# Two-channel stores, smaller early loads and a 5 to 4 split of copies in an im2col kernel

## The chip, the cores and the metric

The kernel runs on one core of a Trainium2 chip. The metric is device microseconds of one execution. A run is "fast" when it was within 1.5% of the fastest run of the same kernel, "slow" when it was longer, and "unknown" when it was the only one. The span in a profile is shorter than the time by about 1.8 us (90.1 and 91.84 us for the same run of the kernel before).

## The reference

```python
x: (16, 64, 32, 32) float32, kernel_size = 3
cols = zeros(16, 64 * 9, 30 * 30)
for b: for i in range(30): for j in range(30):
    cols[b, :, i * 30 + j] = x[b, :, i:i+3, j:j+3].ravel()
```

Each channel of 32 x 32 becomes nine windows of 30 x 30. 4.19 MB are read and 33.18 MB are written; nothing is computed.

## The kernel before

Each of the 128 partitions holds 8 channels, 32 KB in one row of `x`. Loads and stores are done by 16 DMA engines, which move rows between the chip's main memory and the on-chip memory. A channel's nine windows are copied inside the on-chip memory, by VectorE and ScalarE, into an output tile (32.4 KB per channel), and a store writes the tile's row out. Two output tiles of two channels each alternate.

```python
    cuts = [0, H, 200, CPP * H]              # rows: 4, 21 and 7 KB per partition
    first = load(nc.sync, cuts[0], cuts[1])
    bulk = load(nc.sync, cuts[1], cuts[2])
    load(nc.sync, cuts[2], cuts[3])

    on_act = (False, True, False, True, False)
    n = 0
    for c in range(0, CPP, 2):
        out_tile = out_pool.tile([P, 2, KK, HO, WO], x.dtype, name="out_tile")
        for s in range(2):
            for kk in range(KK):
                # ... one copy, on ScalarE or VectorE by on_act[n % 5]
            if c == 0:
                st = nc.sync.dma_start(out=out_v[:, s], in_=out_tile[:, s]...)
                if s == 0:
                    tc.add_manual_dep(st.ins, bulk.ins.name, ...)  # store after the bulk load
        if c > 0:
            nc.sync.dma_start(out=out_v[:, c : c + 2]..., in_=out_tile...)
```

## Time and profile before

| | before |
|---|---|
| median of 3 runs | 91.53 us (91.47 to 92.0) |
| span of the profiled run | 90.1 us |
| DMA engines busy | 97.0% |
| VectorE, ScalarE busy | 26%, 29% |
| first store issued | 10.50 us |
| last of the three loads landed | 12.6 us (issued at 1.2, 11.4 to landing) |

The lines behind it are in the prediction below. They are read as follows: the DMA share is the bound, and what the copying engines do matters only where it decides when a store can be issued.

Beside the profile's views I use the trace's packet records, one for each row that a DMA engine moved (start, duration, bytes) and one of 4 bytes for each engine's completion of a transfer. They carry no engine number. Where I speak of single engines, I joined records in which one starts as another ends. Each of the 16 engines has 8 of the 128 rows of every transfer.

### The profile page before, as it was taken

What the parts mean: (1) busy time and instruction counts of PE and PEld (TensorE: products, weight loads), DVE (VectorE), ACT (ScalarE), POOL (GpSimd) and SP (SyncE); (2) the same over time, 40 slices, a digit from 0 to 9 for tenths busy, and PEclk for the clock granted to TensorE, in tenths of its full rate; (3) what the DMA queues carried; (4) which work ended last, traced back from release to release, by engine and by line L of the source; (5) the groups of instructions that cost most, each with busy time, mean ns of one, the idle gap of its engine ahead of it and who ended that gap; (6) DMA issues with size and microseconds to landing.
All of it is one profiled execution on the core that took longest, in us unless ns stands there. A gap on an engine that the chain in (4) does not pass through costs nothing.

```text
span 90.1 us, 140 instructions
## 1 busy us (share of the span) xinstructions
DVE 23.5 (26%) x43; ACT 26.2 (29%) x30; POOL 0.2 (0%) x4
## 2 busy tenths in 40 slices
DVE  0380399970000089600000399300000000000000
ACT  5391399940000089920000399300000000000000
POOL 0000000000000000000000000000000000000000
DMA  5999899999599999993799999999999999947990
GB/s 129 486 382 449 360 518 446 460 460 446 259 460 460 691 460 432 460 432 173 345 460 460 460 460 460 460 460 460 460 460 460 460 432 460 403 201 345 460 460 0
DMA packets 1152, 37.37 MB, mean 415 GB/s; under 512 B 128, under 2 KB 128, under 8 KB 384
## 3 DMA queue, kind: packets, MB, share of 16 engines
q1 hardware_dynamic: 1152, 37.37, 97.0%
HBM read 4.19 MB, written 33.18 MB: 415 GB/s over the span
## 4 chain that ended last, share of the span: by engine, by line
DMA 45%; DVE 16%; DVEq 1%; issue 0%; SPq 0%
DMA out_dram<-out_tile 35%; DVE out_tile L57 16%; DMA in_tile<-in_x_dram 11%; DVEq L93 1%; DVEq L57 0%; SPq L75 0%
## 5 line engine op out<-in xcount | busy, mean ns | idle before, releaser
L55 ACT COPY out_tile<-in_tile 128x900 f32<-128x900 f32 x29 | 24.9, 938 | 30.1 <-DMA out_dram<-out_tile 25.3
L57 DVE COPY out_tile<-in_tile 128x900 f32<-128x900 f32 x43 | 23.5, 624 | 33.6 <-DMA out_dram<-out_tile 26.0
L55 ACT ACT_TABLE_LOAD x1 | 1.3, 1283 | 0.8 <-PEq L122 0.8
L122 POOL MEMSET const-bfloat16-1.0<- 128x1 bf16 x1 | 0.1, 102 | 0.0
L122 POOL MEMSET const-uint8-127<- 128x1 uint8 x1 | 0.1, 102 | 0.0
L122 POOL MEMSET const-float32-0.0<- 128x1 f32 x1 | 0.1, 99 | 0.2 <-issue 0.2
L122 POOL MEMSET const-float32-1.0<- 128x1 f32 x1 | 0.1, 99 | 0.0
## 6 DMA issues: line engine op xcount, KB each, us to landing
out_dram<-out_tile SPq DMA_DIRECT2D x3, 8100.0 KB, 31.3
out_dram<-out_tile SPq DMA_DIRECT2D x2, 4050.0 KB, 14.9
in_tile<-in_x_dram SPq DMA_DIRECT2D x1, 2688.0 KB, 9.6
in_tile<-in_x_dram SPq DMA_DIRECT2D x1, 896.0 KB, 11.4
in_tile<-in_x_dram SPq DMA_DIRECT2D x1, 512.0 KB, 3.6
```

The lines of the kernel that those rows point to most:

```text
L55: nc.scalar.copy(out=dst, in_=src)
L57: nc.vector.tensor_copy(out=dst, in_=src)
L93: tc.compile()
L122: nc = _bacc.Bacc("TRN2", target_bir_lowering=False, num_devices=1)
```

## The change

The intent is fewer and larger stores, an earlier start of the second channel (so that a first store of two channels can be ready as early as the old one of one channel), and a split of copies that is the same for each channel.

```diff
-    cuts = [0, H, 200, CPP * H]
-    first = load(nc.sync, cuts[0], cuts[1])
-    bulk = load(nc.sync, cuts[1], cuts[2])
-    load(nc.sync, cuts[2], cuts[3])
+    first = load(nc.sync, 0, H)
+    load(nc.sync, H, 2 * H)
+    load(nc.sync, 2 * H, CPP * H)
-    on_act = (False, True, False, True, False)
+    on_act = (False, True, False, True, False, True, False, True, False)
 ...
-            if c == 0:
-                st = nc.sync.dma_start(... one channel ...)
-                if s == 0:
-                    tc.add_manual_dep(st.ins, bulk.ins.name, ...)
-        if c > 0:
-            nc.sync.dma_start(... two channels ...)
+        nc.sync.dma_start(... two channels ...)
```

(Shortened. An assertion on the number of channels is loosened too; it holds here either way.)

More of the change, by code (lines that the diff above doesn't have):

```diff
@@ L19, in _im2col @@
     CPP = B * C // P
-    assert CPP * P == B * C and C % CPP == 0 and CPP % 4 == 0
+    assert CPP * P == B * C and C % CPP == 0 and CPP % 2 == 0
     x_v = x.rearrange("b (cp c2) h w -> (b cp) (c2 h w)", c2=CPP)
@@ L58, in _im2col @@
                 n += 1
-            if c == 0:
-                st = nc.sync.dma_start(
-                    out=out_v[:, s],
-                    in_=out_tile[:, s].rearrange("p kk i j -> p (kk i j)"),
-                )
-                if s == 0:
-                    tc.add_manual_dep(
-                        st.ins,
-                        bulk.ins.name,
-                        mybir.DependencyInfo(
-                            mybir.DependencyClass.Sync, mybir.DependencyReason.DATA
-                        ),
-                        reason="the store follows the bulk of the loads",
-                    )
-        if c > 0:
-            nc.sync.dma_start(
-                out=out_v[:, c : c + 2].rearrange("p c n -> p (c n)"),
-                in_=out_tile.rearrange("p c kk i j -> p (c kk i j)"),
-            )
+        nc.sync.dma_start(
+            out=out_v[:, c : c + 2].rearrange("p c n -> p (c n)"),
+            in_=out_tile.rearrange("p c kk i j -> p (c kk i j)"),
+        )
     return first
```

## The prediction

> **What bounds the kernel now.** I read the page first, for engine shares and DMA. This is the page of the kernel before.
>
> ```profile
> span 90.1 us, 140 instructions
> DVE 23.5 (26%) x43; ACT 26.2 (29%) x30; POOL 0.2 (0%) x4
> ...
> DMA  5999899999599999993799999999999999947990
> ...
> q1 hardware_dynamic: 1152, 37.37, 97.0%
> HBM read 4.19 MB, written 33.18 MB: 415 GB/s over the span
> ```
>
> The two copying engines are busy about a quarter of the span each; the DMA engines 97% of it. The slices marked 5, 3 and 7 in the middle of the DMA row look like holes. To see whether they are, I asked for stretches whose borders I set by the transfers: loads until 11.5, the one-channel stores until 30.7, then one two-channel store per stretch. Columns: stretch, its length, busy time of each engine, clock, DMA share (1.00 is all 16 engines), GB/s.
>
> ```profile
> 0.00:1.00 1.00, 0.00 (x0) 0.21 (x1) 0.20 (x4) 1.00 0.00 0
> 1.00:11.50 10.50, 3.85 (x7) 5.61 (x7) 0.00 (x0) 1.00 1.01 398
> 11.50:21.10 9.60, 8.16 (x16) 7.47 (x9) 0.00 (x0) 1.00 1.01 434
> 21.10:30.70 9.60, 0.00 (x0) 0.00 (x0) 0.00 (x0) 1.00 1.00 432
> 30.70:49.80 19.10, 5.47 (x10) 6.85 (x8) 0.00 (x0) 1.00 1.00 434
> 49.80:69.00 19.20, 6.01 (x11) 6.01 (x7) 0.00 (x0) 1.00 1.00 432
> 69.00:88.20 19.20, 0.00 (x0) 0.00 (x0) 0.00 (x0) 1.00 1.00 432
> 88.20:90.10 1.90, 0.00 (x0) 0.00 (x0) 0.00 (x0) 1.00 0.00 0
> ```
>
> No hole: a packet is counted where it starts, and packets of the big stores last about 2.4 us, so slices of 2.25 us alternate. The share is 1.00 or 1.01 in every stretch from 1.0 to 88.2 us. The time is 1.0 us ahead of the first packet, 87.2 us of full DMA, and 1.9 us for the last packets' ends and the landing. Only bytes, bytes per second, or a new hole can change the sum. The chain of waits names VectorE for 16% of the span, but that is a path through slack: while VectorE copies, the stretch's DMA share is 1.00.
>
> Next, where the copies and issues stand, from the instructions in order of time (start, length, engine and line, names, count, wait before it):
>
> ```profile
> 3.61 3.48 ACT L55 COPY out_tile<-in_tile 128x900 f32<-128x900 f32 x4 [1.54 <-DMA in_tile<-in_x_dram]
> 3.61 2.78 DVE L57 COPY out_tile<-in_tile 128x900 f32<-128x900 f32 x5 [3.61 <-DMA in_tile<-in_x_dram]
> 10.43 8.54 ACT L55 COPY out_tile<-in_tile 128x900 f32<-128x900 f32 x10 [3.35 <-DMA in_tile<-in_x_dram]
> 10.43 9.23 DVE L57 COPY out_tile<-in_tile 128x900 f32<-128x900 f32 x17 [4.04 <-DMA in_tile<-in_x_dram]
> 10.50 3.67 SPq L60 DMA_DIRECT2D out_dram<-out_tile  x2
> 19.74 37.77 SPq L75 DMA_DIRECT2D out_dram<-out_tile  x3
> 31.95 6.85 ACT L55 COPY out_tile<-in_tile 128x900 f32<-128x900 f32 x8 [12.98 <-DMA out_dram<-out_tile]
> 31.97 5.47 DVE L57 COPY out_tile<-in_tile 128x900 f32<-128x900 f32 x10 [12.31 <-DMA out_dram<-out_tile]
> ```
>
> Channel 0 is copied by 7.1 us, but its store waits for the second load and is issued at 10.50. The pair at 31.95 is done in 6.85 us, because ScalarE has 8 copies there; the issue follows about 0.02 us later.
>
> **What the Trainium skill says.** "DMA: Bandwidth & Descriptors", section "Where 436 GB/s comes from": a fabric ceiling of 435 GB/s; the trace's full stretches run at 432 to 434, so this kernel's stores are at it. The same page, "Queues, rings and completion order": on each DMA engine descriptors are consumed in ring order; the trace agrees in that loads are followed by stores at share 1.00, all on one queue, and a store issued ahead merely queues. "ScalarE: Activation LUTs", "What ACT_TABLE_LOAD costs": an activation with immediates takes 186 + 0.833 N ns and neighbours overlap by about 93 ns. For N = 900 that is 936 ns each, 843 ns apart; the trace shows 938 ns on average and (6.85 - 0.94) / 7 = 0.845 us apart. "VectorE: DVE Perf Modes", "Side-by-side": two fp32 elements per cycle plus about 150 cycles, (450 + 150) / 0.96 = 625 ns; the trace shows 624 ns. So both engines' copies are what they should be, and the change alters none of their shapes.
>
> **The change part by part.**
>
> *Bytes and packets.* The bytes stay 37.37 MB. Loads go from 4, 21 and 7 KB per partition to 4, 4 and 24; all remain contiguous rows of at least 4 KB. Stores go from two of 32.4 KB and three of 64.8 KB per partition to four of 64.8 KB. At the traced rate two one-channel stores take 9.60 + 9.60 = 19.20 us, one two-channel store 19.10 to 19.20, so the merge is worth 0 to 0.1 us. Issues fall from 8 to 7 and packets by 144 (128 rows and 16 completion packets), to 1008; on a queue that is full, issuing costs nothing.
>
> *The first store.* This is the one place with little slack. It now needs two channels, 10 VectorE and 8 ScalarE copies. Channel 0 starts at 3.61 as before. The second load is now 512 KB: at 398 GB/s (the load stretch) 1.3 us after the first, so it lands at about 4.9. VectorE reaches channel 1 at 3.61 + 2.78 = 6.39 and ScalarE at 7.09, so neither waits: the stalls of 3.35 and 4.04 us until 10.43 go. ScalarE ends at 3.61 + 6.85 = 10.46 and VectorE at about 3.61 + 5.47 = 9.1. The store is issued at about 10.5, by chance just when the old first store was. When must it be issued to leave no hole? The first load, issued at 0.0, had its first packets just after 1.0 us, so about 1.0 us passes from issue to data. In the kernel before, in half-microsecond stretches:
>
> ```profile
> 11.00:11.50 0.50, 0.50 (x2) 0.50 (x2) 0.00 (x0) 1.00 1.05 444
> 11.50:12.00 0.50, 0.50 (x2) 0.50 (x1) 0.00 (x0) 1.00 2.34 1001
> ```
>
> A 32.4 KB packet takes 1.2 us (9.60 us for 8 per engine), so 2.34 x 0.5 x 16 / 1.2 = 15.6 means that about one store packet started on each of the 16 engines between 11.5 and 12.0: the loads ended there and stores followed at once. An issue at 10.5 gives data at 11.5, so a hole of 0 to 0.1 us. Its cost is one for one, as nothing later catches up.
>
> *The later stores.* The second pair needs the third load, whose bytes end as before and which lands at about 12.6 (1.2 + 11.4 us). Its copies end at 12.6 + 6.85 = 19.5; the first store holds the DMA until 11.5 + 19.15 = 30.7, and the new issue is needed by 29.7. Slack 10 us. The third pair needs the first buffer, free at about 31.95, and is issued at about 38.9 against a need at 48.9; the fourth at about 57.9 against 68.0. All have 10 us to spare.
>
> *The split 5 to 4.* Over the whole kernel VectorE goes from 43 to 40 copies and ScalarE from 29 to 32. At 0.547 us (5.47 / 10) and 0.856 us (6.85 / 8) each that is 21.9 us for VectorE and 27.4 us, plus 1.3 us of table load, for ScalarE. No pair takes over 6.9 us; each has 19 us. Worth nothing after the first store.
>
> *Sum.* 91.53 - 0.05 (fewer packets) + 0.05 (possible hole ahead of the first store) = 91.5 us.
>
> **The rivals.** (1) *The first store comes late.* Tripling the copies ahead of it could starve the DMA after the loads. For it: slack is about zero by the sum above. Against: ScalarE no longer waits for the big second load, and the pair takes a traced 6.85 us. If the second load landed only at 8 us, ScalarE would begin channel 1 then, the store would be issued at 8 + 3.48 = 11.5, and the time would be 92.5. If it were stuck until 10.4 as before, 10.43 + 3.48 = 13.9 gives 3.4 us of hole and 94.9 us. Landing in ring order, which the trace's three landings at 3.6, 10.4 and 12.6 fit, speaks against both.
> (2) *The wait on the loads did work.* The old store was held for the bulk of the loads, as though an earlier store would hurt. If removing it let stores mix with loads, the third load would land late, at worst after the first store, at about 32; the second pair would then be issued at 39, a hole of some 9 us, about 100 us. Against: the new store cannot be issued before 10.5, the very time of the old one, and it queues behind the loads.
> (3) *The stalls removed are gain.* One could take the 3.35 to 4.04 us of engine idling away and predict 88 us. Against: the DMA share in that stretch is 1.01; the engines only idle longer later.
> (4) *Larger stores run faster.* The trace's rates are 432 to 434 for both sizes: at most 0.1 us.
>
> **Range and chances.** The three runs of before span 91.47 to 92.0, so 0.5 us is scatter alone. Rivals 3 and 4 allow a little less, rival 1 up to 1 us more. I take 91.0 to 92.2. A move of 2% is 1.83 us; only rival 2 or the far end of rival 1 reaches it upward, and none downward without more bytes per second: faster 0.01, same 0.96, slower 0.03.
>
> **What would show it.** In the changed kernel's profile: VectorE and ScalarE without a wait between channels 0 and 1; the second load landing before 6.4 us; the first store issued at 10.4 to 10.7; DMA share 1.00 in every stretch from 1.0 to about 88.2; the other issues near 19.5, 38.9 and 57.9; ends of stores 19.1 us apart; 1008 packets; span 89.7 to 90.6. It would be wrong if a stretch near 11.5 had a share well below 1, if the third load landed much later than 12.6, or if the stretches of pure stores ran at other than 432 to 434 GB/s.

## The result, and the profile after

| | before | after |
|---|---|---|
| median, 6 runs each, same rounds | 91.69 us | 92.72 us |
| range | 91.43 to 92.0 | 92.47 to 92.86 |
| span of the profiled run | 90.1 us | 91.0 us |

The ratio is 1.0107, with a 95% interval of 1.0077 to 1.0137. A ratio here is the mean time of one kernel's fast runs over the mean of the other's fast runs of the same rounds, so it is not quite the ratio of the medians. The change is 1% slower: within 2%, but well outside the noise and outside the predicted range.

From the page of the changed kernel:

```profile
span 91.0 us, 133 instructions
DVE 21.9 (24%) x40; ACT 28.7 (32%) x33; POOL 0.2 (0%) x4
...
q1 hardware_dynamic: 1008, 37.37, 96.5%
```

Same bytes, fewer packets, almost the same DMA share. From the instructions of the changed kernel in order of time (columns as in the prediction; later lines cut):

```profile
3.59 6.85 ACT L54 COPY out_tile<-in_tile 128x900 f32<-128x900 f32 x8 [1.52 <-DMA in_tile<-in_x_dram]
3.59 5.46 DVE L56 COPY out_tile<-in_tile 128x900 f32<-128x900 f32 x10 [3.59 <-DMA in_tile<-in_x_dram]
10.46 48.78 SPq L58 DMA_DIRECT2D out_dram<-out_tile  x4
13.58 6.85 ACT L54 COPY out_tile<-in_tile 128x900 f32<-128x900 f32 x8 [3.14 <-DMA in_tile<-in_x_dram]
```

The copies of the first two channels run without a pause and the first store goes out at 10.46 us, as predicted. But the copies of the next pair, which need the third load, start at 13.58 instead of 12.6. The chain of waits of the changed kernel says the same of the load (start, length, what):

```profile
1.17 12.38 DMA in_tile<-in_x_dram
13.56 0.02 issue
```

The third load lands at 13.56 us, 1.0 us later than the third load of before. The copies after it still have 10 us of slack (the next store is issued at 20.46, when the first store has some 11 us to run), so it is not this wait that costs time. It is a sign that the loads themselves took longer. The stretches of the changed kernel with loads, then with pure stores:

```profile
1.00:11.50 10.50, 5.46 (x10) 7.92 (x9) 0.00 (x0) 1.00 1.03 385
...
31.60:50.70 19.10, 5.47 (x10) 6.85 (x8) 0.00 (x0) 1.00 1.00 434
50.70:69.90 19.20, 5.47 (x10) 6.85 (x8) 0.00 (x0) 1.00 1.00 432
```

Before, the same first stretch had a share of 1.01 with 398 GB/s. Now the share is 1.03 with 385 GB/s. A slow packet has a longer record for the same bytes (up to 2407 ns instead of 912, see below), so it raises the share while it lowers the rate. The number to watch is GB/s over share, which is also free of the error of packets cut by the border, since each packet counts in both. At full rate it is 432. In the stretch from 4 to 7 us, before and then after:

```profile
4.00:7.00 3.00, 2.39 (x5) 3.00 (x4) 0.00 (x0) 1.00 0.98 401
```

```profile
4.00:7.00 3.00, 3.00 (x7) 3.00 (x5) 0.00 (x0) 1.00 1.08 369
```

401 / 0.98 = 409 before, 369 / 1.08 = 342 after. The pure stores are unchanged. So the time was lost in the loads, soon after the third one began.

The packet records show the rest. These are the completion packets of each transfer, first and last of the 16 engines, in us:

| | last load done | last store done |
|---|---|---|
| before | 11.53 to 12.21 | 88.16 to 88.77 |
| after | 11.71 to 13.26 | 88.28 to 89.72 |

The fastest engine lost 0.2 us, the slowest 1.05. Every engine has its fixed 8 rows of each store, so the delay of the slowest is carried unchanged to the end: from the last load to the end it takes 89.72 - 13.26 = 76.46 us, against 88.77 - 12.21 = 76.56 before. The merged stores do save 0.1 us. The sum, 1.05 - 0.1 = 0.95, is the difference of the spans (91.0 - 90.1, rounded).

Of the 128 packets of the 24 KB load the typical one took 912 ns, but the longest took 2407; the average excess over 912 was 0.70 us per engine. In the 21 KB load of before it was 0.24. By joined records, eleven engines went from the second load to the third without a pause. The other five were idle first, 2.4 us in all (0.08 to 1.12 us each, as far as the joins tell). The five largest excesses (0.77 to 1.50 us) are in the first packets of these late engines, begun at 4.4 to 5.0 us: 5.6 of the 11.3 us of excess on all engines. The rest is spread over later packets, most of them before 8 us. No engine was idle between the loads and the first store beyond 0.2 us.

### The profile page after: what moved, and what is told of

Read it like the earlier page. It is cut to its first block, busy times and chain, and to the rows that moved or that the text cites. A ratio compares the mean times of both kernels' runs of the same rounds, so it can differ in the third digit from the quotient of the medians.

```text
span 91.0 us, 133 instructions
## 1 busy us (share of the span) xinstructions
DVE 21.9 (24%) x40; ACT 28.7 (32%) x33; POOL 0.2 (0%) x4
## 2 busy tenths in 40 slices
DMA packets 1008, 37.37 MB, mean 411 GB/s; under 512 B 112, under 2 KB 112, under 8 KB 368
## 3 DMA queue, kind: packets, MB, share of 16 engines
q1 hardware_dynamic: 1008, 37.37, 96.5%
## 4 chain that ended last, share of the span: by engine, by line
DMA 48%; ACT 14%; ACTq 1%; SPq 0%; issue 0%
DMA out_dram<-out_tile 35%; ACT out_tile L54 14%; DMA in_tile<-in_x_dram 14%; ACTq L76 1%; SPq L35 0%; ACTq L54 0%
## 5 line engine op out<-in xcount | busy, mean ns | idle before, releaser
L54 ACT COPY out_tile<-in_tile 128x900 f32<-128x900 f32 x32 | 27.4, 939 | 29.4 <-DMA out_dram<-out_tile 24.8
L56 DVE COPY out_tile<-in_tile 128x900 f32<-128x900 f32 x40 | 21.9, 624 | 35.7 <-DMA out_dram<-out_tile 27.5
```

The costliest lines, as they stand in the source:

```text
L54: nc.scalar.copy(out=dst, in_=src)
L56: nc.vector.tensor_copy(out=dst, in_=src)
```

## The experiments

A "call" below is one batch of runs; each has runs of the kernel before in its own rounds, and ratios are to those.

Theory L: the cut of the loads costs it. Rivals: the new stores and copies (S); the copies that now run beside the loads; the length or place of the 24 KB rows; the removed hold on the first store. Later theories (D, E, T, H) are stated where they came up. "Loads done" is first to last engine, from completion packets; "excess" is as above, for the named load. The kernel before had 11.53 to 12.21 and 0.24.

### First call: which part of the change

**The loads of the change in the kernel before.**

```diff
-    cuts = [0, H, 200, CPP * H]
+    cuts = [0, H, 2 * H, CPP * H]
```

> The kernel before with only the row borders of its loads changed to 4, 4 and 24 KB. Theory L (the loss sits in how the loads are cut: the bulk after two small loads reads slower): the last load lands near 13.5 us instead of 12.6 and the time is 1.008 to 1.014 of before. Rival S (the two-channel first store or the 5 to 4 copies cost it): last load lands at 12.6, ratio 0.997 to 1.003.

Ratio 1.0239 (1.0194 to 1.0283), loads done 12.22 to 13.67, third load landed at about 14.0, excess over 912 ns 1.23 us per engine. The stretch of this kernel:

```profile
4.00:7.00 3.00, 3.00 (x7) 3.00 (x5) 0.00 (x0) 1.00 1.12 381
```

381 / 1.12 = 340, as in the changed kernel. The old stores and copies do not protect it, so S alone falls. It lost more than the changed kernel, and more than expected. By start of packet, 0.73 us of the excess lies ahead of 8 us (changed kernel: 0.68) and 0.49 after (changed kernel: 0.03). In this kernel the second load, on which the hold hung, is now tiny, so the first store was issued at 7.07 us, in the middle of the loads. The second part had to have another cause; see the run without the hold.

**Other loads in the changed kernel: 4, 12, 16 KB.**

```diff
-    load(nc.sync, H, 2 * H)
-    load(nc.sync, 2 * H, CPP * H)
+    load(nc.sync, H, 4 * H)
+    load(nc.sync, 4 * H, CPP * H)
```

> The changed kernel with loads of 4, 12 and 16 KB per partition. Channel 1 lands near 7.3 us, so the first store goes out at about 10.8. Theory L in the form 'a second small load is what hurts': last load lands by 12.7 and ratio 0.998 to 1.005. If it is the large last load whatever precedes it: ratio 1.008 or more. Rival S: 1.008 or more.

Ratio 0.9998 (0.9984 to 1.0013), loads done 11.35 to 11.81, excess 0.09 in the second load and 0.00 in the third. The stretch of this kernel:

```profile
4.00:7.00 3.00, 2.43 (x5) 3.00 (x4) 0.00 (x0) 1.00 1.05 436
```

436 / 1.05 = 415. With all other parts of the change in place, another cut of the loads undoes the loss.

**4, 4.5 and 23.5 KB** (cuts at rows 32 and 68).

> The changed kernel with loads of 4, 4.5 and 23.5 KB, so that the rows of the bulk are not whole multiples of 4 KB. If the loss comes from the round size and start of the rows: last load lands near 12.6 and ratio at most 1.003. If from the small second load: near 13.5 and ratio 1.008 to 1.014.

Ratio 1.0037 (0.9997 to 1.0076). In the profile loads were done at 11.23 to 12.26, excess 0.04; one engine was idle for 0.49 us at the start of the third load and ended last. But the spans of its four runs were 90.0, 90.5, 89.6 and 90.3, so one profile is not the whole story: half a kilobyte more in the second load removes part of the loss, not surely all.

**All copies held until the third load has landed** (a dependency of each engine's first copy on that load).

```diff
+                if n < 2:
+                    tc.add_manual_dep(cp.ins, last.ins.name, ...)
```

> The changed kernel with every copy held until the third load has landed. It must lose about 9 us for the hole after the loads. What counts is when the third load lands: 13.5 us if the copies that run beside the loads have no part in the loss, 12.6 if they slow the loads.

Third load landed at 13.15, loads done 11.81 to 12.85, excess 0.72. The stretch of this kernel, with both engines at rest:

```profile
4.00:7.00 3.00, 0.00 (x0) 0.00 (x0) 0.00 (x0) 1.00 1.13 403
```

403 / 1.13 = 357. The slow reads are there without any copy, so the copies are not their cause. (The time, ratio 1.1136, is that of the hole that holding them opens.)

### Second call: length, place, hold

**The 24 KB load as two of 12 KB.**

```diff
-    load(nc.sync, 2 * H, CPP * H)
+    load(nc.sync, 64, 160)
+    load(nc.sync, 160, 256)
```

> The changed kernel with its 24 KB load as two of 12 KB. Theory 'two small loads ahead of the bulk': packets of the third load slow as in the 24 KB one (about 0.7 us per engine in excess of their usual time), loads end near 13.3, ratio 1.008 to 1.014. Theory 'rows of 24 KB are what reads slowly': no slow packets, loads end by 12.3, ratio 0.998 to 1.003.

Ratio 1.0072 (1.0026 to 1.0119), loads done 11.82 to 12.92, excess 0.66 over both 12 KB loads. Long rows are not needed for the loss.

**4, 4, 23.5 and 0.5 KB** (cuts at rows 32, 64 and 252).

> The changed kernel with loads of 4, 4, 23.5 and 0.5 KB: the bulk starts where the 24 KB one does, but its rows are 0.5 KB shorter. If the start of the row counts (8 KB into each 32 KB row): slow as the 24 KB load, ratio 1.008 to 1.014. If the length of the row counts: loads end near 12.5, ratio 1.000 to 1.005 (0.2 us for 128 packets of 512 bytes).

Ratio 1.0107 (1.0051 to 1.0162), excess 0.80 in the 23.5 KB load. The same row length that read fast after 4.5 KB reads slowly after 4 KB. The length is not it.

**4, 8 and 20 KB** (cuts at rows 32 and 96).

> The changed kernel with loads of 4, 8 and 20 KB. If the second load only has to be big enough to keep the engines supplied past 5 us or so: fast, as with 12 KB, ratio 0.998 to 1.003. If long rows at whole KB starts are slow in themselves: 0.3 to 0.7 us of excess in the 20 KB load, ratio 1.004 to 1.010.

Inconclusive. The four runs took 93.46, 91.25, 93.10 and 91.38 us; the two long ones count as slow by the 1.5% rule, and the ratio 0.9952 (0.9884 to 1.0020) is made of the two others alone. The profile fell in a long run: loads were done at 11.44 on the first engine and 13.94 on the last, but the second last by 11.8. One engine was idle for 1.87 us between the first load and the second, and another 0.50 us within the second. It finished 1.4 us after all others at the end. So a single engine that was late in the loads cost the kernel 1.4 us in this run. Whether an 8 KB second load is safe is not shown.

**The kernel before without the hold on its first store.**

```diff
-                if s == 0:
-                    tc.add_manual_dep(st.ins, bulk.ins.name, ...)
```

> The kernel before without the wait that holds its first store for the second load. The store is issued at about 7.1 instead of 10.5 us, behind the loads in the queue. Theory 'queue order protects the loads': ratio 0.998 to 1.002, third load lands at 12.6. Theory 'a store that waits behind the loads slows their reads' (as the late slow packets of the run before with new loads suggest): slow read packets between 7 and 11 us, third load lands at 13.0 to 13.6, ratio 1.005 to 1.012.

Ratio 1.0107 (1.0062 to 1.0151). The store was issued at 7.00 us, and the rows of the last load, 7 KB each, took 441 ns instead of 272 (medians), which is 1.29 us per engine. Loads done 12.70 to 13.08. The stretch from 8 us, in the kernel before and then in this one:

```profile
8.00:12.50 4.50, 2.07 (x4) 2.07 (x3) 0.00 (x0) 1.00 0.95 400
```

```profile
8.00:12.50 4.50, 2.58 (x5) 2.58 (x4) 0.00 (x0) 1.00 0.91 260
```

So the hold was worth 1%. The store did queue behind the loads, since its first packets start at 12.71 us, as the loads end; yet while it waited, the last load read slowly (the 21.5 KB rows ahead of it did not, with an excess of 0.07). How a waiting store does that is not shown. An early store is the likely cause of the late part in the run with the new loads in the kernel before, too; no run took it out there. It is not the cause in the changed kernel, whose first store goes out at 10.46 and whose late excess is 0.03 us.

### Third call: what is special about the third load

Theory D: the third load is needed at about 4 us, before the engines have it.

**8 and 24 KB.**

```diff
-    first = load(nc.sync, 0, H)
-    load(nc.sync, H, 2 * H)
+    first = load(nc.sync, 0, 2 * H)
     load(nc.sync, 2 * H, CPP * H)
```

> The changed kernel with its two 4 KB loads as one of 8 KB. Copies start about 1.3 us later, so the first store is issued at about 11.8 and a hole of about 1 us opens after the loads: ratio 1.008 to 1.014 by that alone. What counts is the 24 KB load, same rows as in the changed kernel. Theory D (the third load of a row of small ones is needed at 4 us before the engines have it; a load issued second has its lead): no idle engine and no slow packets at 4 to 7 us, loads end by 12.3. If the 24 KB rows at 8 KB are slow in themselves: 0.7 us of excess again and loads end near 13.3.

Loads done 11.18 to 11.53, excess 0.01. The stretch:

```profile
4.00:7.00 3.00, 2.37 (x5) 2.37 (x3) 0.00 (x0) 1.00 1.16 500
```

500 / 1.16 = 431, full rate. These are the very rows of the changed kernel's third load, read from 3.9 us on. So neither the rows nor that time of the run are slow in themselves. The first store, issued at 11.51, came too late and every engine was idle for 0.8 to 1.3 us ahead of it; this cut is no remedy. The ratio, 1.0047 (0.9994 to 1.0100), is below the expected 1.008 to 1.014; that fits the end of the loads, 0.7 us earlier than in the kernel before.

**4, 6 and 22 KB** (cuts at rows 32 and 80).

> The changed kernel with loads of 4, 6 and 22 KB, between the 4.5 KB (ratio 1.0037) and the 12 KB (0.9998) that were run. If the loss falls with the length of the second load: ratio 0.999 to 1.004, loads end by 12.4. If 4.5 KB was luck: 1.007 or more.

Ratio 1.0000 (0.9956 to 1.0045), loads done 11.52 to 12.27, excess 0.20. The loss falls with the length of the second load.

**4, 12, 4 and 12 KB** (cuts at rows 32, 128 and 160).

> The changed kernel with loads of 4, 12, 4 and 12 KB: a small load is followed by a larger one again, but at about 8 us, when the larger one was issued long before. Theory D: no stall at 8 us, loads end by 12.3, ratio 0.998 to 1.003. If a small load ahead of a larger one always costs: slow packets from 8 us on, ratio 1.006 or more.

Ratio 0.9981 (0.9921 to 1.0042), loads done 11.36 to 11.72, excess 0.08 over both 12 KB loads. A 4 KB load ahead of a larger one, at 8 us, costs nothing.

**4, 12, 16 KB, the last issued after the first has landed.**

```diff
-    load(nc.sync, 4 * H, CPP * H)
+    late = load(nc.sync, 4 * H, CPP * H)
+    tc.add_manual_dep(late.ins, first.ins.name, ...)
```

> The fast cut 4, 12, 16 KB with the last load issued only when the first has landed, at about 3.6 us, for a need at 6.5: the same lead of about 2.8 us that the 24 KB load has in the changed kernel. Theory D in the form 'a lead of 2.8 us is too short': engines idle or slow at 6.5 to 8 us, loads end at 12.7 or later, ratio 1.005 or more. If lead is not the matter but the early phase or the small loads are: ratio 0.998 to 1.003.

Ratio 0.9971 (0.9913 to 1.0028), loads done 11.21 to 11.84, excess 0.01. A lead of about 2.8 us is enough here, so D in that simple form falls.

### Fourth call: theories E and T

**The changed kernel with its third load issued after the first has landed** (the same dependency).

> The changed kernel with its third load issued only when the first has landed, at about 3.6 us, so that its first packets come at 4.6 or later and every engine idles about 0.4 us. Theory E (the third load suffers because it is taken up while the first two are): no slow packets, loads end within 0.6 us of each other and by 12.6, ratio 1.000 to 1.006. Theory T (any third transfer begun near 4 us suffers): slow packets of 0.4 us per engine or more, loads end at 13.3 to 14, ratio 1.010 to 1.020.

Ratio 1.0096 (1.0037 to 1.0154), excess 0.79, loads done 12.49 to 13.16. By the numbers T is nearer: the packets are slow. But the run does not separate the two as I meant it to. Every one of the 16 engines ran dry, for 0.07 to 1.20 us, and the first packet of every engine took 0.5 to 1.0 us longer than usual. Two stretches of this kernel show the pause and the burst of starts after it:

```profile
3.80:4.60 0.80, 0.80 (x2) 0.80 (x2) 0.00 (x0) 1.00 0.40 159
4.60:5.20 0.60, 0.60 (x2) 0.60 (x2) 0.00 (x0) 1.00 2.83 655
```

What it does show is a cost that I had not reckoned with: an engine that has run dry before a load pays for the idle time and then once more for a slow first packet. The two together, 0.60 us of idle time on average and 0.79 us of excess, were 1.4 us per engine. The first packets of the very first load look alike (0.25 to 0.83 us of excess on 14 engines of the kernel before). It does not take all engines starting at once: the one late engine of the run with 4, 8 and 20 KB, alone in its pause, had a first packet 0.52 us too long. But stores do not pay it: with 8 and 24 KB all engines were idle for about 1 us ahead of the first store, and its first packets took 2.42 to 2.44 us where 2.39 is usual.

**The changed kernel again, for the same chip.**

> The changed kernel itself, for the same chip: ratio 1.007 to 1.013, loads end at 13.0 to 13.6, and again engines idle at 4 to 5 us and first packets of the third load slow.

Ratio 1.0085 (1.0037 to 1.0133), loads done 11.90 to 12.92, excess 0.71, its stretch:

```profile
4.00:7.00 3.00, 3.00 (x7) 3.00 (x5) 0.00 (x0) 1.00 1.09 373
```

373 / 1.09 = 342. The loss repeats in fresh rounds.

**Loads of 4, 4, 4, 4 and 16 KB.**

> The changed kernel with loads of 4, 4, 4, 4 and 16 KB. If each further transfer within the first microseconds costs: ratio 1.010 to 1.020, loads end at 13.3 or later. If only the third transfer does and 4 KB packets at that place are too short to lose much: ratio 1.000 to 1.006.

Ratio 1.0185 (1.0137 to 1.0232), loads done 12.03 to 13.87. The five loads were completed by the last engine at 3.04, 4.97, 6.99, 9.00 and 13.87 us. The 16 KB rows read at full rate (excess 0.02), the 4 KB rows did not (1.29 us per engine over all four loads; the first load alone has about 0.4 to 0.5 in the other kernels). Each further small load in the first microseconds costs more.

**4, 12, 16 KB again.**

> The 4, 12, 16 KB cut again, beside the changed kernel on the same chip: ratio 0.997 to 1.002, loads end by 12.2, no slow packet in the 16 KB load.

Ratio 0.9977 (0.9930 to 1.0024), loads done 11.39 to 11.89, excess 0.00 in the third load and 0.09 in the second. Beside 1.0085 of the changed kernel in the same rounds, the repair holds.

### Fifth call: theory H, a fixed interval per transfer

If transfers were handed to the engines one by one at 1.5 us each, the third would be ready at 4 to 5 us, and all of the above would fit.

**Six loads of 1 KB and one of 26 KB.**

> The changed kernel with six loads of 1 KB per partition and one of 26 KB. A 1 KB load is 8 packets of some 40 to 50 ns per engine, 0.4 us, and the issues are 0.4 us apart. Theory H: the starts of the loads lie about 1.5 us apart, the engines idle most of the first 9 us, the 26 KB load starts near 10 us and the time is above 97 us. If transfers are taken up as fast as they are issued: starts 0.4 to 0.5 us apart, the 26 KB load starts by 4.5 us, the time is below 94 us.

One run each, of unknown state. Time 99.42 us (before in the same round: 91.9). Median packet starts of the six small loads were 1.42, 2.19, 2.70, 3.15, 3.71 and 4.44 us: 0.45 to 0.77 us apart, where the issues are about 0.5 apart. The 26 KB load, issued at about 3.1, had its first packets from 4.15 us on. H's interval of 1.5 us falls for rows of 1 KB. (The time is above 97 us, as expected under H, but for another reason, which I had left out of what I expected: channel 1 lies partly in the 26 KB load, so the first store of two channels came far too late.) The 26 KB load still had an excess of 0.64.

**Three 1 KB rows, each as two transfers of 64 partitions, and 29 KB.**

> Three 1 KB row loads, each as two transfers of 64 partitions, and one of 29 KB: as many transfers as in the run with six 1 KB loads, half the rows in each. If the interval goes by transfer: starts about as far apart as there. If it goes by row: half as far apart, and the 29 KB load starts at about 5.5 us if theory H's 1.5 us holds for 128 rows.

Time 105.14 us. The completions of the six half transfers came at medians of 1.74, 2.78, 3.46, 4.06, 4.74 and 5.37 us, 0.61 to 1.04 apart, while the six issues alone took 4.2 us. So they follow the issues, and neither run shows an interval near 1.5 us. An interval that grows with the length of the rows is not excluded: both runs have 1 KB rows in their small loads, and the question came up with 4 KB. (Channel 0 also lay in the last load here, so the copies started at about 16 us; the time says nothing on the question.)

### All cuts of the loads in one table

| loads, KB per partition | ratio | loads done, us |
|---|---|---|
| 4, 4, 24 | 1.0107; again 1.0085 | 11.71 to 13.26; 11.90 to 12.92 |
| 4, 4, 12, 12 | 1.0072 | 11.82 to 12.92 |
| 4, 4, 23.5, 0.5 | 1.0107 | 12.38 to 12.84 |
| 4, 4, 4, 4, 16 | 1.0185 | 12.03 to 13.87 |
| 4, 4.5, 23.5 | 1.0037 | 11.23 to 12.26 |
| 4, 6, 22 | 1.0000 | 11.52 to 12.27 |
| 4, 8, 20 | two of four runs long | 11.44 to 13.94 in a long run |
| 4, 12, 16 | 0.9998; again 0.9977 | 11.35 to 11.81; 11.39 to 11.89 |

No version beat the kernel before by more than the noise. With the 4, 12, 16 KB cut the change is neutral.

## Why the prediction was wrong

**What bounds the kernel: right.** DMA bytes at 432 to 434 GB/s set the time, and the 10 us of slack later were never used up. The ends of the stores lie 19.1 us apart, as foreseen. The later stores were issued at 20.46, 39.76 and 58.92 us, each 0.9 to 1.0 after the time foreseen, which is the delay of the loads carried on.

**The copies and the first store: right.** No wait between channels 0 and 1, the first store at 10.46 against 10.5 predicted, no hole of note between loads and store, 1008 packets. That there was no hole is in part luck: the loads ended later than foreseen, so the first store was not needed as early as 11.5. Two slips changed nothing: the copies ahead of the first store were doubled (9 to 18), not tripled as rival 1 says, and the 936, 843 and 625 ns for copies are estimates from the pages' formulas, for which the traced 938, 845 and 624 ns decide.

**The merge of stores: right in size**, 0.1 us gained from the last load to the end.

**The step that failed** is in the part on the later stores: "The second pair needs the third load, whose bytes end as before and which lands at about 12.6 (1.2 + 11.4 us)." The prediction had treated the loads as bytes alone ("all remain contiguous rows of at least 4 KB"), so that 4, 4, 24 would take as long as 4, 21, 7. In the changed kernel the third load landed at 13.56, and the slowest engine ended its loads 1.05 us later than before: five engines ran dry ahead of the third load and its packets read slowly until about 8 us. That it is the cut of the loads is shown: with 4, 12, 16 KB and all else of the change, the ratio is 0.9998 and 0.9977.

**The test was named, the reading was too coarse.** The prediction said it would be wrong "if the third load landed much later than 12.6" and that is what happened. But it also expected a loss to show as a share below 1. The share rose; only GB/s fell.

**Rival 2 was half right.** The hold on the first store did work: without it the kernel before is 1.07% slower. The prediction's argument against it was that a store "queues behind the loads", or "merely queues" as it says of the ring order. It does queue, but that run refutes that queueing is harmless to the loads. But in the changed kernel no store is issued while much of the loads is left, so the rival does not explain this loss.

**What stays open** is why a third load that begins at about 4 us finds engines idle and reads slowly, when it was issued 2.8 us before. Ruled out by runs: the copies, the rows' length and place, that time of the run by itself, a small load ahead of a larger one at a later time, a lead of 2.8 us by itself, and (with one run each, of unknown state, and rows of 1 KB) a fixed interval of 1.5 us per transfer. What remains is a description: the four cuts of the table that begin with two loads of 4 KB per partition lost 0.7 to 1.9%, whatever came behind; those with a second load of 6 or 12 KB lost nothing that the intervals show. That an idle engine's next read is slow accounts for about half of the excess in the changed kernel (the five late engines), but not for why they fell idle, nor for the slow packets on engines that did not pause: in the run with 4, 4, 12 and 12 KB three first packets took 1.2 us too long without a pause.

## What to carry to other kernels

Where transfers set the time, look at GB/s over the DMA share, not at the share: a share of 1.0 can hide slow packets. Try a second load with enough bytes to run on for several microseconds (here 12 KB per partition), even if the first must be small to start the engines early. Do not queue stores early behind loads that are still under way: an issue at 7.0 us cost 1% here, one at 10.5 us, one to two microseconds before the loads ended, nothing that was seen. A delay of the slowest DMA engine at the start is a delay of the end, because each engine had its own 8 rows of every later transfer.

## What the Trainium skill lacked or had wrong

- "DMA: Bandwidth & Descriptors", section "Rules for kernel authors", asks for at least 1 MiB per transfer for the best bandwidth. It could have been a warning: the second load of the change has 0.5 MiB, and with 1.5 MiB the loss was gone (0.9998). But the rule does not say where it bites: the loss was gone at 0.75 MiB already (6 KB, ratio 1.0000), and a load of 0.5 MiB in third place, at about 6.5 us, cost nothing (0.9981).
- No page has what a store costs that is queued behind loads: 7 KB read packets of 441 ns instead of 272, 1.1% of this kernel.
- No page has the double cost of an engine that runs dry ahead of a load: 0.60 us idle on average, then a first packet 0.79 us too slow. Ahead of a store the first packet was at most 0.05 us too slow.
- No page says that an engine that is late in one transfer stays late through the next ones: 13.26 us at the end of the loads, 89.72 at the end, against 11.71 and 88.28 on the first engines.
